# The transposes and the accumulating matmuls of a table in one slot instead of three

## The chip, the core and the metric

The kernel runs on one core of a Trainium2 chip. A core has TensorE (PE in the profile, its weight loads PEld), VectorE (DVE), ScalarE (ACT), GpSimd (POOL) and SyncE (SP), each with its own queue of instructions, worked off in order; semaphores join them. The metric is the device time of one execution in microseconds, as the median of several runs.

## The reference, cut to what matters

One inference step of a decoder layer with two halves side by side, for 256 prompt positions and 8 samples of 4 positions (288 token columns in all):

```python
x = x + 0.5 * swiglu(rms_norm(x, ffn1_norm), w_gate, w_up, w_down)   # 2048 -> 5632 -> 2048
z = rms_norm(x, mix_norm) @ w_in                                      # u | q | k | v
y_ssm = s5_mixer(u, ...)      # 64 groups, 64 complex states each, a scan over positions
y_attn = window_attention(q, k, v, ...)
x = x + concat(rms_norm(y_ssm), rms_norm(y_attn)) @ w_out
x = x + 0.5 * swiglu(rms_norm(x, ffn2_norm), ...)
```

The state-space half (SSM) needs matrices that depend on its parameters alone: `lam_bar = exp(lam * dt)`, `B_bar = (lam_bar - 1) / lam * B`, their powers over four positions and the products with `C`. The kernel computes these matrices once per call, for eight tiles of eight groups each; they are called tables here.

## The kernel before, in words

Activations lie transposed: 128 features on the partitions, 288 token columns. Weights come from HBM in pieces of at most 128 x 1024 fp32 numbers. Each piece is split by ScalarE (`wh`, L89, a rounding cast) and VectorE (`wl`, L90, the rest) into two fp32r halves, and each product is made of three matmuls, wh·xh, wh·xl and wl·xh (L273, L274, L275 in `mm3`), all 128 x 128 weights against 288 columns. A gate or up piece holds 8 weight tiles and gives 24 matmuls. A down piece holds 6 (first two chunks, 18 matmuls) or 5 (last two chunks, 15 matmuls).

The order of work around the change is written by `Weights.next` (L103): one call is one **slot**, and stands for one piece. It first issues the split of the piece two ahead, then the load five ahead, then whatever is registered for this slot with `W.at`, and then the caller issues the matmuls of the piece. `W.spread(slot, gen)` runs a generator, one step per slot: each `yield` in it ends a step, and the next step is issued in the next slot.

`precompute(qp)` is such a generator, started at slot 24 while the first feed-forward half (`ffn(0, ...)`, 304 slots: 176 of gate and up pieces, and between them 128 of down pieces in four chunks) runs. After common work it calls `tile_tables(j)` for j = 0 to 7, so everything of table j + 1 follows table j. The part of `tile_tables` that matters here begins with L563: for i = 0 and 1, four transposes on TensorE (L566, fp32, 128 x 128) into a PSUM tile and one ScalarE copy of 128 x 512 into `stage` (L568); then two accumulating fp32 matmuls against 256 columns (L572, `start=i == 0, stop=i == 1`), each of which the trace shows as two instructions. In the next slot ScalarE copies their result out (`kk`, L579). At the end of a table its `stage` is stored to DRAM (`mats[j]`), from which the SSM part loads it after the first half is done. PSUM tiles named `main` come from one pool of eight buffers, for the products, the transposes and these matmuls alike.

Two other places use TensorE with fp32 operands near this part: `norm` (L207, a column sum by a matrix of ones, two instructions) and `gap` (L338, two matmuls of ones against 256 columns whose result is not read; eight slots after the norm of each feed-forward half).

Of the kernel before, what the change touches and what calls it, by code (L numbers as in the profile page):

```python
# [117 lines left out]
def tile_hymba_step(ctx, tc, io):  # L118
# [232 lines left out]
    def precompute(qp):  # L351
# [54 lines left out]
        def frac(f, tmp, hi, lo, nn):  # L406

            tt(f, hi, nn, op=ALU.mult)
            wrap(f, tmp)
            yield  # L410
            tt(tmp, lo, nn, op=ALU.mult)
            tt(f, f, tmp, op=ALU.add)
            yield
            wrap(f, tmp)
            yield

        def cos_sin(c, s, f, tmp):
            act.activation(s, f, AF.Sin, scale=TWO_PI)
            stt(tmp, f, -1.0, f, op0=ALU.mult, op1=ALU.max)
            yield  # L420
            act.activation(c, tmp, AF.Sin, bias=halfpi, scale=-TWO_PI)

        def cmul(outr, outi, ar, ai, br, bi, t, neg=False):

            tt(outr, ar, br, op=ALU.mult)
            tt(t, ai, bi, op=ALU.mult)
            yield
            tt(outr, outr, t, op=ALU.subtract)
            tt(outi, ar, bi, op=ALU.mult)
            yield  # L430
            tt(t, ai, br, op=ALU.mult)
            if neg:
                stt(outi, outi, -1.0, t, op0=ALU.mult, op1=ALU.subtract)
            else:
                tt(outi, outi, t, op=ALU.add)
            yield

        def common():
# [77 lines left out]
            for j in range(8):  # L516
                yield from tile_tables(j)

        def halves(ap):

            return [ap[64 * g:64 * g + 64].rearrange("p q (j g d) -> p q j g d", j=4, g=2)[:, :, :, g, :]
                    for g in range(2)]

        def tile_tables(j):
            q = slice(4 * j, 4 * j + 4)
            bx = [P, 4, 5, 16]
            xr = qp.tile(bx, F32, name="xr")
            xi = qp.tile(bx, F32, name="xi")
            t = qp.tile(bx, F32, name="xt")
            yield from cmul(xr, xi, bc[:, 2, q, None, :].to_broadcast(bx), bc[:, 3, q, None, :].to_broadcast(bx),  # L530
                            erd[:, q, :, None].to_broadcast(bx), eid[:, q, :, None].to_broadcast(bx), t, True)
            for i, src in ((3, xr), (4, xi)):
                for g, dst in enumerate(halves(stage[:, i])):
                    pool_e.tensor_copy(dst, src[64 * g:64 * g + 64, :, 0:4, :])
                yield
            bx = [P, 4, 4, 16]
            br = bb[:, 0, q, None, :].to_broadcast(bx)
            bi = bb[:, 1, q, None, :].to_broadcast(bx)
            pr = er[:, q, 0:4, None].to_broadcast(bx)
            pi = ei[:, q, 0:4, None].to_broadcast(bx)  # L540
            ta, tb, tc_, td = (qp.tile(bx, F32, name=n) for n in ("be0", "be1", "rf", "rtm"))
            tt(ta, br, pr, op=ALU.mult)
            tt(tb, bi, pi, op=ALU.mult)
            yield
            tt(tc_, br, pi, op=ALU.mult)
            tt(td, bi, pr, op=ALU.mult)
            yield
            for g in range(2):
                pp = slice(64 * g, 64 * g + 64)
                tt(bed[0][pp, :, :, g, :], ta[pp], tb[pp], op=ALU.subtract)  # L550
                tt(bed[1][pp, :, :, g, :], tc_[pp], td[pp], op=ALU.add)
                for i in range(2):
                    pool_e.tensor_copy(rep[i][pp, :, g, :], bb[pp, i, q])
                yield
            bx = [P, 4, NCH]
            f = qp.tile(bx, F32, name="rf")
            t = qp.tile(bx, F32, name="rtm")
            yield from frac(f, t, psh[:, q, None].to_broadcast(bx), psl[:, q, None].to_broadcast(bx),
                            nrow[:, None, :].to_broadcast(bx))
            rot = stage[:, 5].rearrange("p q (s k) -> p q s k", s=2)  # L560
            yield from cos_sin(rot[:, :, 0, :], rot[:, :, 1, :], f, t)
            yield
            for i in range(2):  # L563
                ps = pa.tile([P, 512], F32, name="main")
                for q_ in range(4):
                    pe.transpose(ps[:, q_ * P:(q_ + 1) * P],  # L566
                                 bed[i][:, q_].rearrange("p j g c -> p (j g c)"), ident)
                act.copy(stage[:, i].rearrange("p q m -> p (q m)"), ps)  # L568
                yield
            ps = pa.tile([P, 512], F32, name="main")  # L570
            for i, xx in ((0, xr), (1, xi)):
                pe.matmul(ps[:, :256], rep[i].rearrange("p q g c -> p (q g c)"), xx[:, :, 1:5, :],  # L572
                          start=i == 0, stop=i == 1)
            yield
            kk = qp.tile([P, 4, 16], F32, name="kk")
            km = qp.tile([P, 4, 2, 16], F32, name="km")
            for q_ in range(4):
                pp = slice(32 * q_, 32 * q_ + 32)
                act.copy(kk[pp].rearrange("p n d -> p (n d)"), ps[pp, 64 * q_:64 * q_ + 64])  # L579
            yield  # L580
            tt(kk[:, 3], kk[:, 3], de[:, j], op=ALU.add)
            for gi in range(2):
                ts(km[:, :, gi, :], kk, mgi[:, gi:gi + 1], None, op0=ALU.mult)
            yield
            for jr in range(4):
                for q_ in range(4):
                    (act.copy, cp_)[q_ % 2](
                        stage[32 * jr:32 * jr + 32, 2, q_, :32 * jr + 32],
                        km[32 * q_:32 * q_ + 32, 3 - jr:].rearrange("p n g d -> p (n g d)"))
                if jr % 2:  # L590
                    yield
            yield
            act.dma_start(mats[j], stage.rearrange("p a q m -> p (a q m)"))
            yield
            yield
# [675 lines left out]
```

## Time and profile before

| | us |
|---|---|
| median of 3 runs | 1998.82 (1998.45 to 1999.53) |
| the profiled execution, its own time | 1999.87 |
| its span, first to last instruction | 1998.1 |
| TensorE busy in it | 1980.5 (99%) |
| VectorE busy | 1219.0 (61%) |
| ScalarE busy | 852.0 (43%) |
| GpSimd busy | 296.0 (15%) |
| transposes of the tables (L566), first and last start | 217.8 and 688.7 |
| matmuls of the tables (L572), first and last start | 223.5 and 692.7 |
| norm at the end of the first half (L207) | 864.5 |

In rows of the profile, `out<-in` are the program's tile names, `128*128 128x288` is a weight tile of 128 x 128 against 288 columns, and x3136 a count. Matmuls overlap, so the duration of one (some 290 ns) is longer than the distance from its start to that of the next; the pace of TensorE is read from starts or from counts in a window of time.

### The profile page before, as it was taken

The page shows a single profiled execution, that of the slowest core. Times are in us where ns is not written, and L with a number is a line of the kernel's source. Part 1 is how long each engine was busy: PE and PEld are TensorE (multiplying, and loading weights), DVE is VectorE, ACT ScalarE, POOL GpSimd, SP SyncE. Part 2 cuts the span into 40 slices and gives each one's busy share as a digit, 9 for nine tenths or more (in the row PEclk, how much of TensorE's full clock was granted, in tenths as well). Part 3 has the DMA queues.
Part 4 walks back from the last instruction along what each step waited for, and adds up shares of the span by engine and source line. Part 5 has one row for each costly group of instructions (what it writes and reads, how often), then busy time and mean ns, then how long its engine had stood idle before and what let it go on. Part 6 is the DMA issues. An engine that isn't in the chain of part 4 may idle for free.

```text
span 1998.1 us, 37634 instructions
## 1 busy us (share of the span) xinstructions
PE 1980.5 (99%) x15256; PEld 1968.0 (98%) x15256; DVE 1219.0 (61%) x1874; ACT 852.0 (43%) x1334; POOL 296.0 (15%) x450
## 2 busy tenths in 40 slices
PE   8999999999999999999999999999999999999999
PEld 7999999999999999999989999999999999999999
DVE  5577666566666654677888874555555455555554
ACT  5443444443444443543476553333333333333333
POOL 3110011000100000211368640000000000000000
PEclk9999999999999999999999999999999999999999
DMA  7555655546555664678744445555555555555555
GB/s 237 188 169 152 198 168 201 193 151 209 198 180 155 215 201 142 216 248 265 247 132 132 154 159 169 169 155 172 181 169 162 160 186 169 157 157 193 169 154 158
DMA packets 122622, 359.04 MB, mean 180 GB/s; under 512 B 22448, under 2 KB 30256, under 8 KB 121264
## 3 DMA queue, kind: packets, MB, share of 16 engines
q1 hardware_dynamic: 114672, 340.81, 53.5%
q10 hardware_dynamic: 7776, 15.83, 2.3%
q8 instruction: 119, 1.95, 0.4%
q14 instruction: 55, 0.45, 0.1%
HBM read 338.40 MB, written 20.22 MB: 179 GB/s over the span
## 4 chain that ended last, share of the span: by engine, by line
PE 96%; DMA 1%; POOL 1%; DVE 0%; SPq 0%; ACT 0%; issue 0%; POOLq 0%; ACTq 0%; DVEq 0%
PE main L273 31%; PE main L275 31%; PE main L274 31%; POOL acc L191 1%; PE main L733 1%; DMA yd<-yg 0%; PE main L566 0%; PE main L572 0%; DMA x<-in_x 0%; PE main L988 0%; DMA raw<-in_w_gu 0%; PE main L775 0%; PE main L774 0%; PE main L956 0%; PE main L773 0%; PE main L975 0%
## 5 line engine op out<-in xcount | busy, mean ns | idle before, releaser
L90 DVE TENSOR_TENSOR wl<-raw,wh 128x1024 fp32r<-128x1024 f32 (+2 forms) x680 | 758.6, 1116 | 526.2 <-ACT wh L89 521.1
L273 PE MATMUL main<-xh,wh 128*128 128x288 f32 x3136 | 924.4, 295 | 6.7 <-ACT xh L181 6.4
L275 PE MATMUL main<-xh,wl 128*128 128x288 f32 x3136 | 919.0, 293 | 2.2 <-DVE wl L90 2.2
L274 PE MATMUL main<-xl,wh 128*128 128x288 f32 x3136 | 918.4, 293 | 0.6 <-DVE xl L182 0.6
L89 ACT CAST wh<-raw 128x1024 fp32r<-128x1024 f32 (+2 forms) x680 | 643.1, 947 | 600.2 <-PE main L274 385.4
L273 PEld LDWEIGHTS main<-xh,wh 128*128 128x128 f32 x3136 | 589.5, 188 | 8.0 <-ACT xh L181 6.4
L275 PEld LDWEIGHTS main<-xh,wl 128*128 128x128 f32 x3136 | 589.3, 188 | 3.0 <-DVE wl L90 2.9
L274 PEld LDWEIGHTS main<-xl,wh 128*128 128x128 f32 x3136 | 589.5, 188 | 1.4 <-DVE xl L182 1.0
L273 PE MATMUL main<-hh,wh 128*128 128x288 f32 x1664 | 489.8, 294 | 0.0
L274 PE MATMUL main<-hl,wh 128*128 128x288 f32 x1664 | 487.9, 293 | 0.3 <-DVE hl L684 0.3
L275 PE MATMUL main<-hh,wl 128*128 128x288 f32 x1664 | 487.8, 293 | 0.0
L274 PEld LDWEIGHTS main<-hl,wh 128*128 128x128 f32 x1664 | 312.6, 188 | 0.7 <-DVE hl L684 0.5
L273 PEld LDWEIGHTS main<-hh,wh 128*128 128x128 f32 x1664 | 312.5, 188 | 0.5 <-DVE t L1095 0.2
L275 PEld LDWEIGHTS main<-hh,wl 128*128 128x128 f32 x1664 | 312.5, 188 | 0.0
L300 POOL TENSOR_TENSOR s<-s,R 128x288 f32<-128x288 f32 x88 | 71.3, 810 | 1228.0 <-ACT s L299 1228.0
L299 ACT ACTIVATE s<-t 128x288 f32<-128x288 f32 x88 | 39.2, 445 | 233.5 <-DVE t L298 233.5
L309 ACT CAST hh<-h 128x288 fp32r<-128x288 f32 x88 | 38.2, 434 | 235.5 <-DVE h L308 235.5
L330 DVE SCALAR_TENSOR_TENSOR x<-main,x 128x288 f32<-128x288 f32 x128 | 58.4, 456 | 52.3 <-PE main L275 51.1
L308 DVE TENSOR_TENSOR h<-main,s 128x288 f32<-128x288 f32 x88 | 40.2, 457 | 70.3 <-PE main L275 69.9
L298 DVE TENSOR_TENSOR t<-main,R 128x288 f32<-128x288 f32 x88 | 40.2, 457 | 59.4 <-PE main L275 59.2
L310 DVE TENSOR_TENSOR hl<-h,hh 128x288 fp32r<-128x288 f32 x88 | 40.3, 458 | 44.0 <-ACT hh L309 44.0
L191 POOL TENSOR_TENSOR acc<-acc,sq 128x288 f32<-128x288 f32 x45 | 48.4, 1075 | 45.8 <-ACT sq L187 44.4
(266 smaller groups left out, 891.0 us busy)
## 6 DMA issues: line engine op xcount, KB each, us to landing
raw<-in_w_gu SPq DMA_DIRECT2D x352, 512.0 KB, 3.5
raw<-in_w_dn SPq DMA_DIRECT2D x128, 384.0 KB, 3.0
raw<-in_w_dn SPq DMA_DIRECT2D x128, 320.0 KB, 3.0
raw<-in_w_in SPq DMA_DIRECT2D x40, 512.0 KB, 4.7
raw<-in_w_out SPq DMA_DIRECT2D x32, 512.0 KB, 3.4
mats<-stage ACTq DMA_DIRECT2D x8, 1536.0 KB, 7.1
mb<-mats SPq DMA_DIRECT2D x8, 768.0 KB, 5.3
ma<-mats SPq DMA_DIRECT2D x8, 512.0 KB, 4.2
```

What stands on the lines that cost most here:

```text
L89: self.nc.scalar.copy(wh[:, :n], t[:, :n])
L90: self.nc.vector.tensor_tensor(wl[:, :n], t[:, :n], wh[:, :n].bitcast(F32), op=ALU.subtract)
L191: eng.tensor_tensor(acc, acc, sq, op=ALU.add)
L273: pe.matmul(ps, wh[:, s], rh[k], start=first and a == 0, stop=False)
L274: pe.matmul(ps, wh[:, s], rl[k], start=False, stop=False)
L275: pe.matmul(ps, wl[:, s], rh[k], start=False, stop=last and a == n - 1)
L298: dve.tensor_tensor(t1, pg[:, :N], R, op=ALU.mult)
L299: act.activation(s1, t1, AF.Silu)
L300: pool_e.tensor_tensor(s2, s1, R, op=ALU.mult)
L308: dve.tensor_tensor(h, pu[:, :N], s2, op=ALU.mult)
L310: dve.tensor_tensor(hl, h, hh.bitcast(F32), op=ALU.subtract)
L330: dve.scalar_tensor_tensor(x[d], ps[:, :N], 0.5, x[d], op0=ALU.mult, op1=ALU.add)
```

## The change

One `yield` is removed, at the end of the loop over i. Before, the first four transposes and their copy, the second four and their copy, and the two matmuls were issued in three slots that follow one another, with the matmuls of a piece between them. After, all eight transposes, both copies and both matmuls are issued in one slot, ahead of its piece's matmuls. Each table takes two slots less, and so the tables behind the first move to earlier slots. The instructions and their data stay the same.

```diff
             for i in range(2):
                 ps = pa.tile([P, 512], F32, name="main")
                 for q_ in range(4):
                     pe.transpose(ps[:, q_ * P:(q_ + 1) * P],
                                  bed[i][:, q_].rearrange("p j g c -> p (j g c)"), ident)
                 act.copy(stage[:, i].rearrange("p q m -> p (q m)"), ps)
-                yield
             ps = pa.tile([P, 512], F32, name="main")
             for i, xx in ((0, xr), (1, xi)):
                 pe.matmul(ps[:, :256], rep[i].rearrange("p q g c -> p (q g c)"), xx[:, :, 1:5, :],
                           start=i == 0, stop=i == 1)
             yield
```

## The prediction

> **What bounds the kernel now.** I read the page's shares first, then the chain of waits, then a table of time windows, because TensorE was busy throughout and only its pace could still differ.
>
> ```profile
> span 1998.1 us, 37634 instructions
> PE 1980.5 (99%) x15256; PEld 1968.0 (98%) x15256; DVE 1219.0 (61%) x1874; ACT 852.0 (43%) x1334; POOL 296.0 (15%) x450
> PE 96%; DMA 1%; POOL 1%; DVE 0%; SPq 0%; ACT 0%; issue 0%; POOLq 0%; ACTq 0%; DVEq 0%
> ```
>
> The reader is to see that the chain that ends last is 96% TensorE. So a wait that disappears on ScalarE or VectorE is worth nothing here, and a change in the order of TensorE's own instructions is worth what it does to TensorE's pace. The table of windows shows that pace (window in us, length, PE busy time and instructions, granted clock, DMA share, GB/s). A window also counts the two matmuls in flight at its start, so x402 is 400 new ones.
>
> ```profile
> 160.00:212.00 52.00, 52.00 (x402) 1.00 0.51 154
> 230.00:282.00 52.00, 52.00 (x392) 1.00 0.63 212
> 300.00:352.00 52.00, 52.00 (x402) 1.00 0.60 202
> 442.00:487.00 45.00, 45.00 (x339) 1.00 0.66 213
> 506.00:558.00 52.00, 52.00 (x402) 1.00 0.61 201
> 644.00:684.00 40.00, 40.00 (x302) 1.00 0.72 230
> 700.00:752.00 52.00, 52.00 (x402) 1.00 0.61 202
> 217.81:864.48 646.67, 646.67 (x4928) 1.00 0.58 189
> ```
>
> TensorE has two paces for the same 288-column matmul, both at clock 1.00 and both without a gap: 52/400 = 130.0 ns, and 52/390 = 40/300 = 133.3 ns. The slow pace is not the DMA's doing: 0.61 of the DMA engines goes with 130 and 0.63 with 133. The pace changes only where something other than a 288-column matmul has just run, and in this stretch those are the transposes (L566) and the accumulating pairs (L572) of the eight tables. They fall at 218, 284, 361, 431, 491, 568, 634 and 685 us. Tables 1, 4 and 7 leave TensorE at 133.3 until the next table; tables 2, 3, 5, 6 and 8 leave it at 130.0. That is what the change can move.
>
> **What a block does to the pace.** In the slow pace every fourth matmul takes longer. Durations in ns (min/median/max) tell the paces apart: the first row is a stretch at 130, the second the slot right behind four transposes that came out of the pace of 130; then two groups of four transposes and the first matmul of three pairs.
>
> ```profile
> L274 PE MATMUL main<-xl,wh x134: 291/292/293, 300.0 to 351.8; 128*128 128x288 f32 x134
> L274 PE MATMUL main<-hl,wh x6: 292/293/302, 218.4 to 220.4; 128*128 128x288 f32 x6
> L566 PE MATMUL main<-ident,bed x4: 271/272/273, 217.8 to 218.1; 128*128 128x128 f32 x4
> L566 PE MATMUL main<-ident,bed x4: 273/273/273, 684.8 to 685.1; 128*128 128x128 f32 x4
> L572 PE MATMUL main<-xr,rep x2: 379/379/379, 223.5 to 223.7; 128*128 128x256 f32 x2
> L572 PE MATMUL main<-xr,rep x2: 377/377/377, 291.6 to 291.8; 128*128 128x256 f32 x2
> L572 PE MATMUL main<-xr,rep x2: 377/377/377, 638.7 to 638.9; 128*128 128x256 f32 x2
> ```
>
> So transposes put TensorE into the slow pace (302 appears behind them and never in the fast stretch), and whether the pair gets it out again depends on how the pair is entered. The timeline (start us, us) around the pair of table 2, which ends fast, and of table 1, which ends slow:
>
> ```profile
> 291.02 0.30 PE L275 MATMUL main<-xh,wl 128*128 128x288 f32 x1
> 291.16 0.29 PE L273 MATMUL main<-xh,wh 128*128 128x288 f32 x1
> 291.29 0.29 PE L274 MATMUL main<-xl,wh 128*128 128x288 f32 x1
> 291.42 0.29 PE L275 MATMUL main<-xh,wl 128*128 128x288 f32 x1
> 291.55 0.59 PE L572 MATMUL main<-xr,rep 128*128 128x256 f32 x2
> 292.22 0.48 PE L273 MATMUL main<-xh,wh 128*128 128x288 f32 x1
> 292.55 0.29 PE L274 MATMUL main<-xl,wh 128*128 128x288 f32 x1
> 292.67 0.29 PE L275 MATMUL main<-xh,wl 128*128 128x288 f32 x1
> ...
> 223.18 0.30 PE L274 MATMUL main<-hl,wh 128*128 128x288 f32 x1
> 223.32 0.29 PE L275 MATMUL main<-hh,wl 128*128 128x288 f32 x1
> 223.46 0.59 PE L572 MATMUL main<-xr,rep 128*128 128x256 f32 x2
> 224.13 0.48 PE L273 MATMUL main<-hh,wh 128*128 128x288 f32 x1
> 224.45 0.29 PE L274 MATMUL main<-hl,wh 128*128 128x288 f32 x1
> 224.58 0.29 PE L275 MATMUL main<-hh,wl 128*128 128x288 f32 x1
> ```
>
> The long matmul (0.30) stands three matmuls further back in the first, and just one further back in the second: the pair of table 2 starts at the fourth place of the slow beat, that of table 1 at the second. Behind it the second matmul is followed after 0.12 us in table 2 and after 0.13 in table 1. The place is set by the number of matmuls in the slot since the transposes: 24 in a gate or up slot (fourth place, durations that begin at 377, fast), 18 in a down slot of the first chunks (379 throughout, slow), 15 in a later down slot (377, but slow). A 377 at the start is needed and not enough.
>
> **The change, part by part.** The removed yield moves both groups of four transposes, their two ScalarE copies and the pair into one slot. No instruction is added or dropped.
>
> ```profile
> 217.97 0.44 PE main L566 x4
> 223.62 0.86 PE main L572 x4
> L568 ACT COPY stage<-main x16: 572/581/590, 218.7 to 690.4; 128x512 f32<-128x512 f32 x16
> 217.92 0.83 ACT L89 CAST wh<-raw 128x768 fp32r<-128x768 f32 x1 [1.09 <-issue]
> 220.75 0.83 ACT L89 CAST wh<-raw 128x768 fp32r<-128x768 f32 x1 [1.50 <-issue]
> ```
>
> - TensorE's own work stays: 64 transposes at 0.44/4 = 0.109 us are 7.0 us, and 32 matmul instructions of the pairs at 0.86/4 = 0.215 us are 6.9 us. Difference 0.
> - Ends of blocks: three per table become one. From the last transpose into the pair no row exists; bounds are 0.109 us (transpose to transpose) and 0.33 us (292.22 to 292.55, the longest distance behind a pair). I take the pair's own 0.215, since within a block each instruction takes its own length. Either way it is 8 x 0.1 us, so -0.8 to +0.9.
> - ScalarE has two copies in one slot, 1.16 us beside a cast of 0.83. What hides it: a slot here is 2.8 us (217.92 to 220.75, the casts of two slots), the merged one about 1.3 us longer, and the cast stands ahead of the copies in ScalarE's order. Cost 0. Without that cover the next cast, and so the next wh, would be up to 0.6 us late, at most 8 x 0.6 = 4.7 us.
> - PSUM: three tiles of eight are taken in one slot instead of one each in three; a main product takes one tile in two slots, so the eighth tile back was taken some ten slots earlier and read soon after its two slots. 0.
> - Tables: two yields less each, so the last comes 14 slots earlier and the mats store too; its first reader runs after 864 us. 0.
> - The pace. 4928 - 2 - 96 = 4830 matmuls of 288 columns stand between the first transposes and the norm at 864.48. All at 130.0 ns they are 627.9 us, with the 13.9 above 641.8: the kernel before, at 646.67, loses 4.9 us. All at 133.33 they are 644.0, so 657.9: 11.2 us more than before. The change ranges over -4.9 to +11.2.
>
> Which of the two? After the change a pair is no longer entered from a beat of matmuls whose place varies with the slot, but always from the eighth transpose. [...] Besides, a block that ends after transposes has always left matmuls at 133.3, from whichever pace it was entered. I therefore forecast that **all eight tables leave TensorE at 133.3 ns**, from 218 us up to the norm: 1998.82 + 11.2 = 2010.0 us. The sum is made on an execution of span 1998.1 and own time 1999.87, 0.05% over the median; I add it to the median.
>
> **Rivals.**
> 1. *The pair always resets.* Coming in a fixed way, it might always be entered well, like the five tables that end fast. Then the stretch is 641.8: 1998.8 - 4.9 = 1993.9. For it: five of eight pairs, and the same form (L338, two matmuls of 256 columns) resets the pace at 1201 us. Against it: those were all entered from the fourth place, none from transposes. This is the other side, and it decides at one point: the first pair matmul beginning at 377 and the second matmul behind it following after 0.12 us. Chance 0.20.
> 2. *Tables differ,* because the entry keeps a trace of the slot's kind. Half fast, half slow is 641.8 to 657.9 in the middle, about 2002, from 1996 to 2008. Chance 0.07.
> 3. *The pace does not answer to the order:* 0 difference, 1998.8. The windows speak against it, as pace changes only at blocks. Chance 0.04. The Trainium skill's "TensorE: Matmul & The Clock Gate", Back-to-back issue gap, gives one spacing for one size, N/2.4 + 2.5 ns, by which 288 columns would take an estimated 122.5 ns; by that rule the order could not matter, and this trace's 130.0 and 133.3 at one clock disagree with it.
> 4. *The clock drops.* If a run of 0.87 us of transposes made the granted clock fall for one slot of 3.1 us (24 x 130 ns) per table, that would be 8 x 3.1 = 25 us: 2024. Chance 0.02, since the clock stands at 1.00 in the window that holds all the blocks, 217.81 to 864.48. The same page, in PE-mode transpose, says that transposes do not count as busy for the gate; this speaks against the change, and no row here shows a drop behind four of them.
> 5. *The later reset is lost.* The block L338 at 1201 takes the pace from 133 to 130 for all that follows:
>
> ```profile
> 1177.00:1200.00 23.00, 23.00 (x174) 1.00 0.47 155
> 1210.00:1262.00 52.00, 52.00 (x402) 1.00 0.51 164
> ```
>
> If it were entered at another place of the beat, the rest, some 6100 matmuls (793 us/0.130), would cost 3.33 ns each, 20 us on top of the forecast: 2030. Between 865 and 1120 us TensorE waits for others and starts its beat anew, so I give it 0.03.
>
> **How the numbers follow.** The forecast has 0.64: its own range is 2008 to 2012 (the block ends, and the 1.1 us over which the runs before lie). With rivals 2 and 3 that is 0.75, so the range has to take in rival 1: 1993 to 2012. About 0.2% (4 us) is what a measurement of this kernel tells from no change. Rival 1 lies at -0.24%, so of its 0.20 I count 0.15 faster and 0.05 the same; of rival 2 0.02, 0.02 and 0.03; rival 3 the same; forecast and rivals 4 and 5 slower. Faster 0.17, same 0.11, slower 0.72.
>
> **What would show it.** Windows of 52 us behind tables 2, 3 and 5, 6 with x392 where they had x402; one run of eight transposes of about 0.87 us per table, the pair right behind it with 379 from the first; the norm of L207 near 875.7 us instead of 864.5. Wrong is the forecast if the pair begins at 377 and x402 follows every table (norm near 859.6), if x392 and x402 alternate, or if TensorE shows waits between 218 and 864 us.

## The result

The changed kernel takes 2011.26 us in the median (2010.50 to 2012.53, four runs) against 1998.63 us for the kernel before, which ran beside it (1997.96 to 1999.53, four runs). The ratio is 1.0064 with a 95% interval of 1.0051 to 1.0076: **slower by 12.6 us**. Forecast were 2010.0 us and a range of 1993 to 2012. The profiled execution took 2010.50 us, its span is 2008.7 us; before, 1999.87 and 1998.1.

The first rows of the page of the changed kernel, and the shares of the chain that ended last:

```profile
span 2008.7 us, 37635 instructions
PE 1992.1 (99%) x15256; PEld 1979.2 (99%) x15256; DVE 1219.1 (61%) x1874; ACT 852.0 (42%) x1334; POOL 298.5 (15%) x450
PE 96%; DMA 2%; POOL 1%; DVE 1%; SPq 0%; ACT 0%; issue 0%; ACTq 0%; POOLq 0%; DVEq 0%
```

Nothing was added: the same 15256 matmul records, the same number of instructions on VectorE and ScalarE, and TensorE still makes up 96% of the chain. But TensorE is busy 11.6 us longer, 1992.1 for 1980.5. The table of windows of the changed kernel (window, length, PE busy and instructions, clock, DMA share, GB/s) says where:

```profile
160.00:212.00 52.00, 52.00 (x402) 1.00 0.51 156
222.00:274.00 52.00, 52.00 (x392) 1.00 0.61 205
292.00:344.00 52.00, 52.00 (x392) 1.00 0.59 193
362.00:414.00 52.00, 52.00 (x392) 1.00 0.57 182
480.00:532.00 52.00, 52.00 (x392) 1.00 0.61 208
552.00:604.00 52.00, 52.00 (x392) 1.00 0.59 194
680.00:732.00 52.00, 52.00 (x392) 1.00 0.62 208
217.38:875.23 657.85, 657.85 (x4929) 1.00 0.58 186
1222.00:1274.00 52.00, 52.00 (x402) 1.00 0.53 165
```

Ahead of the first table there are 400 matmuls in 52 us, as before. In each of the six windows behind tables (1, 2, 3, 5, 6 and 8) there are 390, also behind those that left 400 before, and so it stays until the norm; the block `gap` at 1211.9 us then brings back 400. The stretch from the first transposes to the norm has grown from 646.67 to 657.85 us, by 11.18, while the spans differ by 10.6. So in these two executions the rest of the kernel is within 0.6 us of what it was; the 1.4 us by which the runs differ further are inside the interval.

One table's block, first as pieces of the chain of waits (start, us), then in the timeline of TensorE:

```profile
217.54 0.87 PE main L566 x8
218.42 0.87 PE main L571 x4
```

```profile
217.38 1.03 PE L566 MATMUL main<-ident,bed 128*128 128x128 f32 x8
218.25 0.60 PE L571 MATMUL main<-xr,rep 128*128 128x256 f32 x2
218.69 0.59 PE L571 MATMUL main<-xi,rep 128*128 128x256 f32 x2
218.93 0.48 PE L273 MATMUL main<-hh,wh 128*128 128x288 f32 x1
219.25 0.29 PE L274 MATMUL main<-hl,wh 128*128 128x288 f32 x1
219.38 0.29 PE L275 MATMUL main<-hh,wl 128*128 128x288 f32 x1
219.51 0.29 PE L273 MATMUL main<-hh,wh 128*128 128x288 f32 x1
219.64 0.29 PE L274 MATMUL main<-hl,wh 128*128 128x288 f32 x1
219.78 0.29 PE L275 MATMUL main<-hh,wl 128*128 128x288 f32 x1
219.91 0.30 PE L273 MATMUL main<-hh,wh 128*128 128x288 f32 x1
```

The eight transposes take 0.87 us and the pair 0.87 us, just what the parts took apart (0.44 + 0.44 and 0.86). The loss is not in the block. It comes after it: the second matmul behind the pair is followed after 0.13 us, and at 219.91 a matmul of 0.30 stands, which the pace of 130 does not have. Durations in ns (min/median/max) of the block of table 3, and of matmuls that follow table 2:

```profile
L566 PE MATMUL main<-ident,bed x8: 270/273/273, 349.6 to 350.4; 128*128 128x128 f32 x8
L571 PE MATMUL main<-xr,rep x2: 379/380/382, 350.5 to 350.7; 128*128 128x256 f32 x2
L571 PE MATMUL main<-xi,rep x2: 379/379/379, 350.9 to 351.2; 128*128 128x256 f32 x2
L274 PE MATMUL main<-xl,wh x131: 292/294/302, 291.8 to 343.8; 128*128 128x288 f32 x131
```

No matmul of the pair takes 377 now: in all eight tables the first takes 382, which no pair of the kernel before took. And the 302 of the slow beat fills the stretch behind table 2, which had 291/292/293 before.

### The profile page after: what moved, and what is told of

Read it like the earlier page. It is cut to its first block, busy times and chain, and to the rows that moved or that the text cites. A ratio compares the mean times of both kernels' runs of the same rounds, so it can differ in the third digit from the quotient of the medians.

```text
span 2008.7 us, 37635 instructions
## 1 busy us (share of the span) xinstructions
PE 1992.1 (99%) x15256; PEld 1979.2 (99%) x15256; DVE 1219.1 (61%) x1874; ACT 852.0 (42%) x1334; POOL 298.5 (15%) x450
## 4 chain that ended last, share of the span: by engine, by line
PE 96%; DMA 2%; POOL 1%; DVE 1%; SPq 0%; ACT 0%; issue 0%; ACTq 0%; POOLq 0%; DVEq 0%
PE main L273 31%; PE main L275 31%; PE main L274 31%; POOL acc L191 1%; DMA yd<-yg 1%; DMA U<-ud 0%; PE main L732 0%; DMA x<-in_x 0%; PE main L566 0%; PE main L571 0%; PE main L987 0%; PE main L955 0%; PE main L974 0%; DMA raw<-in_w_gu 0%; PE main L773 0%; PE main L774 0%
```

## The experiments

All times below from "the first transposes to the norm" come from one profiled execution each; the sum over a stretch in which TensorE never waits repeats closely (657.85, 657.73, 657.86 and 657.79 us in four different kernels).

### Which part of the merge does it

First, the transposes are left together, and the pair alone moves back to the next slot.

```diff
                 act.copy(stage[:, i].rearrange("p q m -> p (q m)"), ps)
+            yield
             ps = pa.tile([P, 512], F32, name="main")
```

> Eight transposes and both copies in one slot, the pair of matmuls one slot later. Theory (entry): the pace that a table leaves is set by how the pair is entered, that is by the number of 288-column matmuls between the last transpose and the pair: 24 gives 130.0 ns, 18 and 15 give 133.3, none gives 133.3. The eight tables then have 18, 24, 24, 18, 18, 24, 15, 15 between (each table one slot shorter than before), so tables 2, 3 and 6 leave 130 and the others 133.3: 652.8 us from the first transposes to the norm (before 646.7, changed kernel 657.9), about 6 us over the kernel before in all. Rival (ScalarE and PSUM): two copies and two PSUM tiles in one slot slow TensorE: as the changed kernel, 657.9. Rival (a run of eight transposes is to blame): 657.9 too.

Measured: 2003.94 us in the median beside 1998.73 (ratio 1.0023, 1.0014 to 1.0033), and 651.62 us in the stretch, 1.2 less than expected. The first row is the stretch; then come windows behind tables 1 to 8 in their order:

```profile
216.42:868.04 651.62, 651.62 (x4929) 1.00 0.58 187
222.00:274.00 52.00, 52.00 (x392) 1.00 0.63 207
292.00:344.00 52.00, 52.00 (x402) 1.00 0.60 202
362.00:414.00 52.00, 52.00 (x402) 1.00 0.55 182
428.00:476.00 48.00, 48.00 (x362) 1.00 0.62 199
486.00:538.00 52.00, 52.00 (x392) 1.00 0.58 194
562.00:614.00 52.00, 52.00 (x402) 1.00 0.53 174
628.00:666.00 38.00, 38.00 (x295) 1.00 0.67 208
680.00:732.00 52.00, 52.00 (x392) 1.00 0.61 201
```

Seven tables are as the count of matmuls says: 18 between gives 133.3 (52/390, 48/360), 24 gives 130.0, and table 8 with 15 has 133.3. Table 7 is not: it has 15 between and runs at 38/293 = 130 ns. Its timeline ahead of the pair shows why.

```profile
624.41 0.30 PE L275 MATMUL main<-hh,wl 128*128 128x288 f32 x1
624.55 0.29 PE L273 MATMUL main<-hh,wh 128*128 128x288 f32 x1
624.68 0.29 PE L274 MATMUL main<-hl,wh 128*128 128x288 f32 x1
624.81 0.29 PE L275 MATMUL main<-hh,wl 128*128 128x288 f32 x1
624.94 0.59 PE L572 MATMUL main<-xr,rep 128*128 128x256 f32 x2
```

The long matmul stands fourth from the end: here 15 matmuls lead to the fourth place. In table 8 (its pair starts at 671.58) the long one stands third from the end, so there 15 lead to the third place. The beat began differently behind the two groups of transposes: the first long matmul is the 12th behind those of table 7 and the ninth behind those of table 8. The pace behind a pair goes with its place, and the count is only a way to it. The two copies of ScalarE and the run of eight transposes are in this kernel as in the changed one, and it still gets 6.2 of the 11.2 us of the loss back.

The other half of the merge: the pair behind the second four transposes, the first four in a slot of their own.

```diff
                 act.copy(stage[:, i].rearrange("p q m -> p (q m)"), ps)
+                if i == 0:
+                    yield
             ps = pa.tile([P, 512], F32, name="main")
```

> The first four transposes in a slot of their own with their copy, the second four with the pair in the next slot. Theory (entry): the pair is entered right behind a transpose in all tables, so every table leaves 133.3: 657.9 us from the first transposes to the norm, 11 to 13 us over the kernel before. Rival (ScalarE and PSUM) and rival (a run of eight): both are undone here, so 646 to 653 us, at most 6 us over the kernel before.

Measured: 2009.82 us beside 1998.73 (ratio 1.0052, 1.0037 to 1.0067), and the whole loss in the stretch:

```profile
215.47:873.20 657.73, 657.73 (x4928) 1.00 0.58 186
```

Eight in a row and two copies in a slot are undone here, and nothing is gained. What is left of the merge is the pair right behind a transpose.

### The slots of the tables

Two yields at the end of a table bring each back to its slot of the kernel before.

```diff
                           start=i == 0, stop=i == 1)
             yield
+            yield
+            yield
             kk = qp.tile([P, 4, 16], F32, name="kk")
```

> The change with two idle steps at the end of each table, so that all tables begin in the slots of the kernel before (24 slots apart). Theory (entry): 657.9 us from the first transposes to the norm, 11 to 13 us over the kernel before. Rival (slots): if it were the earlier slots of the tables, or the share of gate and down slots that they meet, the time is that of the kernel before, 646.7.

Measured: 2009.38 us beside 1998.73 (ratio 1.0049, 1.0034 to 1.0064).

```profile
216.14:874.00 657.86, 657.86 (x4929) 1.00 0.58 186
```

The moved tables have no part in it.

### No blocks at all

```diff
-            for i in range(2):
-                ps = pa.tile([P, 512], F32, name="main")
-                for q_ in range(4):
-                    pe.transpose(...)
-                act.copy(stage[:, i].rearrange("p q m -> p (q m)"), ps)
-            ps = pa.tile([P, 512], F32, name="main")
-            for i, xx in ((0, xr), (1, xi)):
-                pe.matmul(...)
+            yield
+            yield
             yield
...
-                act.copy(kk[pp].rearrange("p n d -> p (n d)"), ps[pp, 64 * q_:64 * q_ + 64])
+                act.copy(kk[pp], xr[pp, q_, 1:5, :])
```

> Leaves out the transposes, their copies and the pair of all tables (what follows is copied from another tile, so the SSM half is not computed); the number of slots per table is that of the kernel before. Theory (entry): nothing is left in this stretch that could change the pace, so all 4830 matmuls run at 130.0 ns: 627.9 us between the same two places, and 1998.6 - 18.8 = 1979.8 us in all; every window of 52 us counts x402. Rival (load of the other engines or DMA makes the slow stretches): they stay, and only the 13.9 us of the blocks' own work goes: 632.8 us, 1984.7 in all.

Measured: 1981.1 us (ratio 0.9913, 0.9897 to 0.9930). The same windows that held 390 and 300 in the kernel before, and the stretch from `gap` to the norm, which was 793.40 us there (71.08 to 864.48):

```profile
230.00:282.00 52.00, 52.00 (x403) 1.00 0.66 213
644.00:684.00 40.00, 40.00 (x310) 1.00 0.66 206
69.46:844.09 774.63, 774.63 (x5958) 1.00 0.60 191
```

The stretch is shorter by 18.77 us, 13.9 of the blocks' own work and 4.9 of pace. With DMA shares of 0.66 TensorE runs at 130.0 here, so neither the load nor the engines beside it made the slow stretches: the blocks do.

### Choosing the place of the pair

In the next three the eight transposes stay in one slot, and the pair is issued after a fixed number of 288-column matmuls, counted in `mm3`; 24, 26 or 28.

```diff
     def mm3(ps, wh, wl, kts, rh, rl, first, last):
...
             pe.matmul(ps, wh[:, s], rh[k], start=first and a == 0, stop=False)
+            tick()          # after each of the three; counts down, then issues the pair
...
-            ps = pa.tile([P, 512], F32, name="main")
-            for i, xx in ((0, xr), (1, xi)):
-                pe.matmul(ps[:, :256], ...)
+            due.append([24, pair])
             yield
+            while not box:
+                yield
+            ps = box[0]
```

> Eight transposes in one slot as in the change, but the pair is issued after 24 matmuls of 288 columns have followed them, whatever the slot (in a slot of 18 or 15 that is inside the next one). Theory (place): what decides is the place of the slow four-beat at which the pair is entered, and 24 matmuls behind eight transposes it is the fourth, so the six tables that stand in slots of 24 and 18 leave 130.0 ns, among them tables 1, 4 and 5, which stand in slots of 18. In the two last tables, in slots of 15, the last experiment but three had another place, so they are open: 641.8 us from the first transposes to the norm if they are fast too, 643 if table 7 alone is slow, 648 if table 8 is. In all 1994 to 2000 us beside 1998.7. Rival (kind of slot: pairs in slots of down pieces leave TensorE slow because of their operands): tables 1, 4, 5, 7 and 8 slow, 652 us or more.

> As with 24, but 26 matmuls between the transposes and the pair in every table. Theory (place): two places on, the pair meets the beat as 18 did, and the six tables in slots of 24 and 18 leave 133.3: 652 to 658 us from the first transposes to the norm. Rival (time: the pair works if it comes late enough behind the transposes): fast as with 24, 642 to 648.

> As with 24, but 28 matmuls between. Theory (place): a whole beat on, the same place as with 24, so the six tables in slots of 24 and 18 leave 130.0: 642 to 648 us from the first transposes to the norm. Rival (24 is special because it ends a slot): slow, 652 to 658.

Measured: with 24, 1999.91 us beside 1998.65 (ratio 1.0005, 0.9996 to 1.0014: no difference); with 26, 2008.96 and with 28, 1995.61, one run each. Rows of the three kernels, 24 first, then 26, then 28:

```profile
216.10:863.42 647.32, 647.32 (x4928) 1.00 0.59 189
490.00:540.00 50.00, 50.00 (x387) 1.00 0.59 194
680.00:732.00 52.00, 52.00 (x392) 1.00 0.57 190
```

```profile
216.18:873.97 657.79, 657.79 (x4929) 1.00 0.58 186
```

```profile
217.42:860.90 643.48, 643.48 (x4928) 1.00 0.59 190
680.00:732.00 52.00, 52.00 (x402) 1.00 0.62 210
```

Two matmuls more turn 647 into 658, two further ones turn that into 643. So neither the distance in time nor the end of a slot counts; a whole beat of four leaves the pair fast in most tables, half a beat makes all slow. The kind of slot is not it either: table 5 stands in a slot of 18 and leaves TensorE at 130 with 24 between (50/385). With 24, table 8 alone stays slow (52/390), and 647.32 is what was expected for that. With 28 it is another table, the seventh (285 in 38 us from 626 to 664). Both times the long matmul is the last one ahead of the pair, which is the first place, and the first long one behind the transposes is the 12th, as in table 7 of the first experiment; in the other tables of these two kernels it is the ninth.

All three tables follow a slot of 15 matmuls and come out of the pace of 130, but that is not enough: table 8 of the first experiment does so too and has the ninth. What goes with the shift in the traces is the number of 288-column matmuls between the pair before (`gap` for table 1) and the transposes. It is odd in the three (501, 321 and 497), and even in every other table of these experiments where eight transposes come out of 130 and matmuls stand ahead of the pair. No run changes that number by itself, so it is a reading and not shown.

The place says nothing of a pair with no matmul ahead of it. Nought is a multiple of four like 24 and 28, and yet the pair right behind transposes left TensorE at 133.3 in all 24 tables of the changed kernel and the second and third experiments.

### The pair ahead of the transposes

```diff
+            ps = pa.tile([P, 512], F32, name="main")
+            for i, xx in ((0, xr), (1, xi)):
+                pe.matmul(...)
             for i in range(2):
-                ps = pa.tile([P, 512], F32, name="main")
+                pt = pa.tile([P, 512], F32, name="main")
...
-            ps = pa.tile([P, 512], F32, name="main")
-            for i, xx in ((0, xr), (1, xi)):
-                pe.matmul(...)
             yield
```

> The same slot as in the change, with the pair ahead of the eight transposes. Theory (place): transposes always leave 133.3, so the pair's place does not matter and all eight tables leave 133.3: 657.9 us from the first transposes to the norm (658.8 from the first pair, with its 0.9 us). Rival (it is the pair right behind the transposes that does the harm): the time of the kernel before or better, 642 to 647.

Measured: 2009.46 us in one run, and from the first pair to the norm

```profile
217.00:874.84 657.84, 657.84 (x4929) 1.00 0.57 186
```

All tables are slow, as expected; the sum there counted the first pair twice (657.9 holds it already). In all eight tables here, transposes that end the block leave TensorE in the slow pace, with the pair ahead of them. The harm is thus not done by the pair behind the transposes: it fails to undo theirs.

### A version that beats both

Table 8 gets 27 matmuls between, as 15 led to the fourth place in table 7 of the first experiment, and 27 is three beats more.

```diff
-            due.append([24, pair])
+            due.append([27 if W.pieces[W.slot - 1].shape[-1] == 5 * P else 24, pair])
```

> As with 24 between the transposes and the pair, but 27 where the slot ahead of the transposes is one of 15 (table 8 alone). Theory (place): behind a slot of 15 the beat starts at another place, where 15 matmuls led to the fourth, and so 15 + 12 = 27 do; table 8 leaves 130.0 too, as the other seven do with 24. All eight fast: 641.8 us from the first transposes to the norm, 4.9 less than the kernel before and 16 less than the change; about 1994 us beside 1998.7. Rival (a pair in or behind a slot of 15 cannot be placed so): table 8 stays slow, 647.3.

Measured: 1994.67 us beside 1999.06 (ratio 0.9978, 0.9969 to 0.9987), and

```profile
217.41:859.76 642.35, 642.35 (x4929) 1.00 0.59 190
490.00:542.00 52.00, 52.00 (x402) 1.00 0.61 199
680.00:732.00 52.00, 52.00 (x402) 1.00 0.59 199
```

The stretch is 4.3 us shorter than before and 15.5 shorter than in the changed kernel. The expected 641.8 left out that the matmuls between transposes and pair stay in the slow pace, an estimated 8 x 24 x 3.33 ns = 0.64 us; the stretch is 0.6 us over it.

This version also closes the count of places. In the kernel before and the five experiments with matmuls ahead of the pair (the first, 24, 26, 28 and this one) there are 48 pairs. The 31 whose long matmul stands fourth from the end all leave TensorE at 130.0 ns; the 17 where it stands last (3), second (12) or third (2) from the end all leave it at 133.3.

## Why the prediction was right, point by point

- *TensorE is the bound, and only its pace can change.* Right: no wait of TensorE appears between 80 and 870 us in either kernel, and 11.18 us of pace stand against 10.6 us in the span.
- *The work of the blocks stays.* Right: 0.87 and 0.87 us. From the last transpose to the pair I took 0.215 us; it is 0.11 (the transposes start at 217.38, 0.109 apart, so the eighth at 218.14, and the pair starts at 218.25). That was inside the bounds, and it did not move the sum.
- *ScalarE, PSUM and the earlier tables cost nothing.* Right, and shown twice over: without them the loss stays (second and third experiment), with the first two of them it is halved (first experiment).
- *Entered from the eighth transpose, the pair leaves TensorE at 133.3.* Right in what was forecast, in all eight tables. The sign was not quite as forecast: the pair begins at 382 and not at 379, so this entry is none of those that the kernel before had. What the runs show is that a pair right behind transposes does not undo the pace that they leave (second and third experiment, and the pair ahead of them); why it does not is open, and the rule of the place, found later, would not have given it.
- *The sum.* 657.9 us forecast for the stretch, 657.85 measured. The total was 1.3 us over the forecast of 2010.0, and the upper bound of 2012 was close, with the slowest of the four runs, 2012.53, above it: the runs of the two kernels differ by 1.4 us more than this stretch.
- *"The place is set by the number of matmuls in the slot since the transposes."* This step was too simple. It holds for 18 and 24 in the kernel before, where the 15 of table 7 led to the third place, at 377 and slow. But 15 also led to the fourth place in the first experiment, and 24 and 28 missed in one table each. How the transposes are entered counts too.
- *The rivals.* That the pair always resets, and that the tables differ, are out with all eight slow. That the order does not matter is out by the 14 us between 26 and 28. The clock did not drop: 1.00 over 217.38 to 875.23, with eight transposes in a row. The Trainium skill's "TensorE: Matmul & The Clock Gate", PE-mode transpose, has it that transposes do not count as busy for the gate in the same way; no run here shows an effect of that. The later reset was not lost: 402 in the window behind `gap`. The estimate of 122.5 ns beside the third rival took a rule too far: the Trainium skill's "TensorE: Matmul & The Clock Gate", Back-to-back issue gap, calls N/2.4 + 2.5 ns the gap of an isolated matmul and has other figures for a stream of weight loads and matmuls. This kernel is such a stream, with as many weight loads as matmuls (x15256 each), so its 130.0 and 133.3 ns do not speak against that formula.

What stays open is why a place in the beat decides, and why a pair right behind transposes changes nothing. The trace shows starts and durations, not what inside TensorE repeats with four matmuls.

## What to carry to other kernels

Where TensorE is busy throughout, read its pace as a count of equal matmuls in equal windows, stage by stage, and look at what ran just before a pace changed: here a 2.6% slower pace, invisible in the busy share and the clock, lasted from one small block to the next. Removing a scheduling step that costs nothing by itself can change how such a block is entered, so a merge of small foreign operations into a stream of equal matmuls is to be judged by the stream behind it and not by the block. If a pace can be chosen, it is worth a try to shift the last foreign operation by one, two or three matmuls.

## What the runs showed of the hardware that was not expected

The distance of a few matmuls has a large effect: pairs 24, 26 and 28 matmuls behind the transposes give 647.3, 657.8 and 643.5 us for the same work. A pace, once entered, lasts: in the changed kernel 133.3 ns held for the whole 213 us from the last table to the norm (from 662 to 875 us), through changes of slot, evictions and transfers, and in the kernel without blocks 130.0 ns held for 775 us.
